# The last product of a decoder layer on one core: seven products of sums in place of direct rank-256 updates

## The chip, the cores and the metric

The kernel runs on one core of a Trainium2 chip. The metric is the device time of one execution in microseconds (us); of several runs the median counts. Data are 32-bit floats. TensorE works on pairs of a rounded high part and a low remainder ("hi" and "lo"): each product of two tiles is three matmuls, hi·hi, hi·lo and lo·hi.

## The reference, cut to what matters

One decoder layer over 1024 tokens of width 1024: two gated mixers (dilated attention and a spatial gating unit) with an output projection `w_out`, cross-attention into a memory, then a SwiGLU feed-forward layer and a final norm. The change concerns the feed-forward layer's second product, with D_FF = 2816:

```python
f = rmsnorm(h, g_ffn[l])
gt, up = jnp.split(f @ w_gate_up[l], 2, axis=-1)
h = h + (jax.nn.silu(gt) * up) @ w_down[l]
return rmsnorm(h, g_final)
```

## The kernel before

The 2816 hidden units are 22 blocks of 128 (`NJ`, index j). For every j the hidden tile `silu(gate)*up`, 128 units x 1024 tokens, is made and sent to DRAM (`hm_d`). Block 0 is made by plain products (`ff_plain`, L1309), the other 21 by `wino` (L416) with the class `Hidden` (L1328): seven products of sums of quarters (Strassen in Winograd's form), 12 matmuls of 512 columns each. The callbacks c11, c22, c12 and c21 turn the PSUM banks into the two halves of the tile `hmf` (tokens 0 to 511 and 512 to 1023); c12 (L1340) finishes the first half, c21 (L1350) the second, and then one DMA of SyncE's queue (SP) stores the tile (L1348).

`down` (L1357) then multiplies by `w_down`. It goes in nine groups of two hidden blocks and a last one of four (`FF_GROUPS`, L318). Of each block the hidden tile and 128 rows of the weight come through the staging pool `wst` (three buffers, L147), ScalarE (ACT) writes the hi part and VectorE (DVE) the lo part (`split`, L136 to L140). For each of 8 blocks of 128 tokens and each half of the 1024 columns, `mm3` (L166 to L171) accumulates a group in one PSUM bank, and a DVE addition adds it to the residual `h` (L1383). The last group adds the squares, the final norm and the stores (L1385 to L1402).

Tiles of 4 KB a partition come from `heap` (20 buffers), of 8 KB from `big` (8 buffers), split weights from `whl` (4 hi and 4 lo buffers). In the hidden stage `heap` holds 12 tiles of operand sums, three weight tiles for each of two blocks in work, and the `hmf` tiles.

The order of each engine's instructions is set by a scheduler ahead of time, which places what its model takes as ready. `keep_in_program_order` pins an instruction behind everything already traced on its engine. Each engine then works strictly in that order, and so do the DMA queues of SP, ACT and GpSimd (POOL): a DMA that waits holds up those behind it.

Two earlier places matter. `out_proj` (L1136) multiplies by `w_out`: its eight row blocks are loaded by SP through `wst` and split, and POOL loads eight tiles of `x` (L1143, pinned). After them POOL has nothing to do until the last group of `down` (L1362).

Of the kernel before, what the change touches and what calls it, by code (L numbers as in the profile page):

```python
# [85 lines left out]
def tile_hybrid_dilated_attn_sgu_gated_block(  # L86
# [169 lines left out]
    def plan_w(*items):  # L256
        plan.extend(items)
# [19 lines left out]
    def rows(w, k):  # L277
        return lambda: load_split([w[0, k * P:(k + 1) * P, :][:, None, :]], (1, 1024))
# [39 lines left out]
    FF_GROUPS = [(j, j + 1) for j in range(0, NJ - 4, 2)] + [tuple(range(NJ - 4, NJ))]  # L318
    hm_d = dram.tile([NJ, P, S], F32, name="hm_d")
    h_d = dram.tile([NT, P, D], F32, name="h_d")  # L320

    def ff_hidden(j):
        def go():
            t = BIG("hm", (P, 2, S))
            return load_split([hm_d[j][:, None, :]], (1, S), (t[:, 0], t[:, 1]))
        return go
# [3 lines left out]
    for js in FF_GROUPS:  # L330
        for jj in js:
            plan_w(ff_hidden(jj), rows(w_down, jj))

# [975 lines left out]
    def ff_plain(j):  # L1309
        wg, wu = next_w(0), next_w(0)  # L1310
        t = H("hmf")
        for half in range(2):
            order.join("f%d" % half)
            if half == 1:
                ready_w.append(next(start_w()))
                sums(lambda name, kk: raw_f[name][kk], "S1")
            hs = slice(half * HALF, (half + 1) * HALF)
            ps = []
            for w in (wg, wu):
                ps.append(PS("psg"))  # L1320
                yield from mm3(ps[-1], [(w[0][:, k], w[1][:, k], a_k(half, 0, k), a_k(half, 1, k))
                                        for k in range(NK)], T512)
                if w is wg:
                    nc.scalar.activation(t[:, hs], ps[0], AF.Silu)
            nc.vector.tensor_mul(t[:, hs], t[:, hs], ps[1])
        nc.sync.dma_start(hm_d[j], t)

    class Hidden:  # L1328
        def __init__(self, j):
            self.j = j  # L1330
            self.t = H("hmf")

        def c11(self, a):
            nc.scalar.activation(self.t[:, :HALF], a, AF.Silu)
# [5 lines left out]
        def c12(self, u, c):  # L1340
            nc.vector.tensor_add(u, u, c)
            nc.vector.tensor_mul(self.t[:, :HALF], self.t[:, :HALF], u)
            self.put()

        def put(self):
            self.n = getattr(self, "n", 0) + 1
            if self.n == 2:
                nc.sync.dma_start(hm_d[self.j], self.t)  # L1348

        def c21(self, p1, b):  # L1350
            t = self.t[:, HALF:]
            nc.vector.tensor_add(p1, p1, b)
            nc.scalar.activation(t, p1, AF.Silu)
            nc.vector.tensor_mul(t, t, self.up)
            self.put()

    def down(js, final=False):  # L1357
        if final:
            ng = H("ng")
            ap = bass.AP(tensor=g_final.tensor, offset=g_final.offset, ap=[[0, P], [1, D]])  # L1360
            tc.keep_in_program_order(nc.scalar.dma_start(ng, ap))
            nc.gpsimd.tensor_scalar(ng, ng, -1.0, None, op0=ALU.mult)  # L1362
        if js[0] == 0:
            for tb in range(NT):
                h[tb] = H("h")
                nc.sync.dma_start(h[tb], h_d[tb])
        wd = []
        for jj in js:
            hm[jj] = next_w(2)
            wd.append(next_w(2))  # L1370
        for tb in range(NT):
            ts = slice(tb * P, (tb + 1) * P)
            if final:
                y = H("y")
                ss = small.tile([P, 8], F32, name="ss", tag="ss")
            last = final and tb == NT - 1
            pieces = ((0, 512), (512, 256), (768, 256)) if last else ((0, 512), (512, 512))
            for i, (c0, n) in enumerate(pieces):
                ns = slice(c0, c0 + n)
                ps = PS("psd")[:, :n]  # L1380
                yield from mm3(ps, [(hm[j][0][:, 0, ts], hm[j][1][:, 0, ts], w[0][:, 0, ns], w[1][:, 0, ns])
                                    for j, w in zip(js, wd)], n / 512 * T512)
                nc.vector.tensor_add(h[tb][:, ns], h[tb][:, ns], ps)  # L1383
                if final:
                    nc.scalar.activation(y[:, ns], h[tb][:, ns], AF.Square, accum_out=ss[:, i:i + 1])  # L1385
            if not final:
                continue
            nc.vector.tensor_add(ss[:, 4:5], ss[:, 0:1], ss[:, 1:2])
            if last:
                nc.vector.tensor_add(ss[:, 4:5], ss[:, 4:5], ss[:, 2:3])  # L1390
            r = neg_rsqrt(ss[:, 4:5], 1)
            for n in range(2):
                ns = slice(n * 512, (n + 1) * 512)
                if last:
                    nc.vector.scalar_tensor_tensor(y[:, ns], h[tb][:, ns], r[:, 0:1], ng[:, ns],
                                                   op0=ALU.mult, op1=ALU.mult)
                    nc.sync.dma_start(out[0, tb * P:(tb + 1) * P, ns], y[:, ns])
                else:
                    nc.scalar.activation(y[:, ns], h[tb][:, ns], AF.Copy, scale=r[:, 0:1])
                    nc.gpsimd.tensor_mul(y[:, ns], y[:, ns], ng[:, ns])  # L1400
            if not last:
                nc.sync.dma_start(out[0, tb * P:(tb + 1) * P, :], y)  # L1402

    def main():
        yield from start()
        x_sums()
        yield from proj_v(2)
        yield from wino_rows(SV())
        for g, pr in QK_PAIRS:
            yield from wino(QK(g, pr))  # L1410
        for j in (0, 2):
            yield from wino(Act(AF.Gelu_apprx_tanh, (u_d[j], u_d[j + 1])))
        for j in range(GATES):
# [24 lines left out]
        order.join("combine")  # L1438
        yield from branch_attn()
        yield from out_proj()  # L1440
        yield from q_proj(0)
        spawn_cross(0)
        yield from q_proj(1)
        order.join("x0")
        spawn_cross(1)
        yield from cross_out(0)
        yield from cross_out(1)
        yield from ff_plain(0)
        for j in range(1, NJ):
            yield from wino(Hidden(j), plain_first=j == 1)  # L1450
        for js in FF_GROUPS:
            yield from down(js, final=js is FF_GROUPS[-1])

    order.run(main())

# [56 lines left out]
```

## Time and profile before

| | us |
|---|---|
| median of 3 runs | 1520.75 (1517.08 to 1521.48) |
| the profiled execution | 1518.75 |
| its span, first to last instruction | 1517.0 |
| PE busy | 1484.5 (98%) |
| DVE busy | 972.6 (64%) |
| ACT busy | 555.5 (37%) |
| POOL busy | 95.4 (6%) |

The mean granted clock of TensorE is 0.991 of full speed. The profiled execution is 1.75 us longer than its span and 2.0 us under the median. A busy share is an average over stages; which wait ends last has to be read stage by stage. "PE" are the matmuls, "PEld" the loads of the stationary operand beside them.

### The profile page before, as it was taken

The numbers are of one execution on the slowest core, as the hardware profiler recorded it, in microseconds if no ns is written. First come the engines' busy times: TensorE is split into PE (matmuls) and PEld (weight loads), VectorE is DVE, ScalarE is ACT, GpSimd is POOL, SyncE is SP. The second block draws the span as 40 slices with busy tenths as digits, with TensorE's granted clock in tenths as the row PEclk, the third lists the DMA queues.
The fourth block names the chain that finished last, engine by engine and source line by source line (L and its number), as shares of the span: only waits on it lengthen the run. The fifth ranks groups of instructions, "written<-read, shape, count | busy, mean of one in ns | idle before, by whom it ended". The sixth has DMA issues, their size and how long they took to land.

```text
span 1517.0 us, 19581 instructions
## 1 busy us (share of the span) xinstructions
PE 1484.5 (98%) x7567; PEld 1244.8 (82%) x7567; DVE 972.6 (64%) x1789; ACT 555.5 (37%) x1028; POOL 95.4 (6%) x107
## 2 busy tenths in 40 slices
PE   8999999999998999899999999999999999999997
PEld 8899888888886777788888888888888888888886
DVE  7786555555456848626677995555555546766666
ACT  4245233333346851215456732222222222211124
POOL 5300000000012203000000000000000000000014
PEclk9999999999999999999999999999999999999999
DMA  6223333333396429300111232222222226332312
GB/s 213 66 90 119 111 111 111 111 111 111 112 310 225 171 86 307 123 1 13 57 56 70 84 102 84 84 81 84 83 83 82 83 98 251 122 99 85 97 56 98
DMA packets 135634, 168.54 MB, mean 111 GB/s; under 512 B 7742, under 2 KB 108850, under 8 KB 135412
## 3 DMA queue, kind: packets, MB, share of 16 engines
q1 hardware_dynamic: 122304, 125.04, 25.7%
q0 software_dynamic: 8096, 29.13, 5.7%
q10 hardware_dynamic: 5140, 13.11, 2.5%
q8 instruction: 59, 0.97, 0.3%
q14 instruction: 35, 0.29, 0.1%
HBM read 125.17 MB, written 42.09 MB: 110 GB/s over the span
## 4 chain that ended last, share of the span: by engine, by line
PE 87%; DVE 5%; DMA 4%; ACT 2%; issue 1%; POOL 0%; SPq 0%; DVEq 0%; ACTq 0%; POOLq 0%
PE psb L412 20%; PE psc L412 13%; PE psg L412 13%; PE psd L171 5%; PE psd L169 5%; PE psd L170 5%; PE pso L171 3%; PE pso L169 3%; PE pso L170 3%; PE psv L170 1%; PE psv L169 1%; PE psv L171 1%; PE psb L491 1%; DMA wbc<-wt_d 1%; DMA wst<-in_w_in_dram 1%
## 5 line engine op out<-in xcount | busy, mean ns | idle before, releaser
L137 ACT ACTIVATE wh<-wst 128x1024 fp32r<-128x1024 f32 x134 | 140.3, 1056 | 411.4 <-PE psg L412 245.8
L140 DVE TENSOR_TENSOR wl<-wst,wh 128x1024 fp32r<-128x1024 f32 x130 | 160.8, 1240 | 80.3 <-ACT wh L137 80.0
L412 PE MATMUL psg<-A,wh 128*128 128x512 f32 x592 | 182.4, 389 | 0.0
L1383 DVE TENSOR_TENSOR h<-h,psd 128x512 f32<-128x512 f32 (+1 forms) x161 | 108.1, 681 | 60.0 <-PE psd L171 59.8
L171 PE MATMUL psd<-wh,hm 128*128 128x512 f32 (+1 forms) x356 | 137.6, 387 | 0.0
L170 PE MATMUL psd<-wl,hm 128*128 128x512 f32 (+1 forms) x356 | 137.6, 387 | 0.0
L169 PE MATMUL psd<-wh,hm 128*128 128x512 f32 (+1 forms) x356 | 137.5, 387 | 0.0
L412 PEld LDWEIGHTS psg<-A,wh 128*128 128x128 f32 x592 | 111.0, 188 | 23.0
L412 PE MATMUL psg<-A,wl 128*128 128x512 f32 x296 | 115.1, 389 | 0.0
L412 PE MATMUL psc<-S,t 128*128 128x512 f32 x444 | 106.6, 389 | 0.0
L412 PEld LDWEIGHTS psc<-S,t 128*128 128x128 f32 x444 | 83.3, 188 | 17.3
L412 PE MATMUL psc<-S,wh 128*128 128x512 f32 x296 | 91.4, 390 | 0.0
L412 PE MATMUL psb<-S,wh 128*128 128x512 f32 x296 | 91.2, 389 | 0.0
L412 PE MATMUL psb<-S,t2h 128*128 128x512 f32 x296 | 91.1, 389 | 0.0
L412 PE MATMUL psb<-A,t2h 128*128 128x512 f32 x288 | 88.7, 389 | 0.0
L433 DVE TENSOR_TENSOR u<-p,psb 128x512 f32<-128x512 f32 x37 | 25.4, 686 | 92.9 <-PE psb L412 92.9
L170 PEld LDWEIGHTS psd<-wl,hm 128*128 128x128 f32 x356 | 66.8, 188 | 14.1 <-DVE wl L140 0.3
L171 PEld LDWEIGHTS psd<-wh,hm 128*128 128x128 f32 x356 | 66.9, 188 | 13.6
L169 PEld LDWEIGHTS psd<-wh,hm 128*128 128x128 f32 x356 | 66.8, 188 | 13.5
L436 DVE TENSOR_TENSOR v<-p,psc 128x512 f32<-128x512 f32 x37 | 25.4, 686 | 64.1 <-PE psc L412 64.1
L137 ACT ACTIVATE t2h<-wst 128x1024 fp32r<-128x1024 f32 x37 | 39.3, 1061 | 72.1 <-DVE wst L398 53.7
L412 PEld LDWEIGHTS psg<-A,wl 128*128 128x128 f32 x296 | 55.6, 188 | 11.6
(344 smaller groups left out, 3270.9 us busy)
## 6 DMA issues: line engine op xcount, KB each, us to landing
wst<-in_w_gate_up_dram SPq DMA_DIRECT2D x44, 512.0 KB, 4.0
wst<-in_w_in_dram SPq DMA_DIRECT2D x42, 512.0 KB, 4.7
hm_d<-hmf SPq DMA_DIRECT2D x22, 512.0 KB, 4.4
wst<-hm_d SPq DMA_DIRECT2D x22, 512.0 KB, 3.4
wst<-in_w_down_dram SPq DMA_DIRECT2D x22, 512.0 KB, 3.7
sig_d<-act ACTq DMA_DIRECT2D x16, 512.0 KB, 3.4
xin<-in_x_dram SPq DMA_DIRECT2D x8, 512.0 KB, 8.6
wst<-in_w_kv_cross_dram SPq DMA_DIRECT2D x8, 512.0 KB, 5.0
```

The source lines that it names most:

```text
L137: i = nc.scalar.activation(hi, src, AF.Copy)
L140: (eng or nc.vector).tensor_sub(lo, src, hi.bitcast(F32))
L169: nc.tensor.matmul(ps, lhsT=lh, rhs=rh, start=(i == 0), stop=False)
L170: nc.tensor.matmul(ps, lhsT=lh, rhs=rl, start=False, stop=False)
L171: nc.tensor.matmul(ps, lhsT=ll, rhs=rh, start=False, stop=(i == n - 1))
L412: nc.tensor.matmul(ps, lhsT=l, rhs=r, start=first and k == 0 and i == 0, stop=k == 3 and i == 2, skip_group_check=not first)
L433: nc.vector.tensor_add(u, p1, b)
L436: nc.vector.tensor_add(v, p1, c)
L491: nc.tensor.matmul(p, lhsT=l, rhs=r, start=first and t % 2 == 0 and k == 0 and i == 0, stop=k == 3 and i == 2, skip_group_check=not first ...
L1383: nc.vector.tensor_add(h[tb][:, ns], h[tb][:, ns], ps)
```

## The change

The hidden matrix A (1024 tokens x 2816) and `w_down` (2816 x 1024) are cut into quarters. The contraction's halves are the even and the odd hidden blocks (11 each, `KP`), the others are the two halves of the tokens ("lo_", "hi_") and of the output columns. Seven products of sums replace the eight direct ones. Each product is one stage of 11 steps over its whole contraction, in four PSUM banks (one for each 128 tokens); a step has 4 x 3 matmuls of 512 columns.

- Sums of hidden quarters are made by DVE: one subtraction at each odd block of the hidden stage (`Hidden.put`), for which the even block's tile is kept in `heap` for one block longer; the others in `prep` of the stages 0, 2 and 3.
- Sums of weight quarters (T1 to T4) are made in DRAM by 32 DMAs of POOL's queue, pinned behind `out_proj`: 16 plain copies and 16 that add to what is there. A sum of 2.75 MiB goes in four pieces of three or two blocks.
- Hidden tiles and `h` are loaded by POOL's queue, straight to SBUF; SP loads two weight blocks at a time. `prep` splits the operands; up to four steps are kept ready (`whl` has four buffers).
- The banks are read by `into`, in part after later stages have begun (`todo`, two calls a step). Two stages go on accumulating in the banks of an earlier one.
- `hm_d` is stored in halves, four DMAs of 256 KB for each pair of blocks.

```diff
-        nc.sync.dma_start(hm_d[j], t)
+            if half == 0:
+                nc.sync.dma_start(hm_d[j][:, hs], t[:, hs])
+        hm[j] = t
...
+        def put(self, half):
+            hs = slice(half * HALF, (half + 1) * HALF)
+            j = self.j
+            if half == 0 or j % 2:
+                nc.sync.dma_start(hm_d[j][:, hs], self.t[:, hs])
+            if half == 1 and j % 2:
+                e = hm.pop(j - 1)
+                nc.vector.tensor_sub(e[:, hs], e[:, hs], self.t[:, hs])
+                nc.sync.dma_start(hm_d[j - 1][:, hs], e[:, hs])
...
+    def down_sums():
+        for dst, src in (("T3", "W22"), ("T1", "W11"), ("T3", "W12"), ("T1", "W12"), ("T2", "T3"), ("T2", "W11"),
+                         ("T4", "T2"), ("T4", "W21")):
+            for k0, k1 in ((0, 3), (3, 6), (6, 9), (9, KP)):
...
+                tc.keep_in_program_order(nc.gpsimd.dma_start(
+                    wsum_d[dst][k0:k1].rearrange("k p c -> p k c"), s_, **({} if first_ else {"accum_op": ALU.add})))
...
+        place(0, (0, 1, 2), False)
+        place(0, (3, 4, 5, 6), True)
+        place(0, (7, 8, 9, 10), False)
+        place(1, (0, 1, 2, 3), True)
+        for tb in range(NT):
+            h[tb] = H("h")
+            nc.gpsimd.dma_start(h[tb], h_d[tb])
+        place(1, (4, 5, 6, 7), True)
+        place(1, (8, 9, 10), False)
...
+        stages = ((even, lo_, "W11"), (odd, lo_, "W21"), (even, lo_, "T2"), (even, hi_, "T1"), (odd, lo_, "W22"),
+                  (even, lo_, "T3"), (odd, hi_, "T4"))
...
+            split(a, hi[:, :HALF], lo[:, :HALF])
+            split(w, hi[:, HALF:], lo[:, HALF:])
...
+            if s_ == 0:
+                nc.vector.tensor_sub(e[:, lo_], e[:, hi_], e[:, lo_])
+            elif s_ == 2:
+                nc.vector.tensor_add(o[:, lo_], o[:, lo_], e[:, lo_])
+            elif s_ == 3:
+                nc.vector.scalar_tensor_tensor(e[:, lo_], o[:, hi_], -1.0, e[:, lo_], op0=ALU.mult, op1=ALU.subtract)
...
+                while n_prep < min(n0 + 4, len(steps)):
+                    prep(n_prep)
+                    n_prep += 1
+                for _ in range(2):
+                    if todo:
+                        todo.pop(0)()
+                for t in range(4):
+                    ts = slice(t * P, (t + 1) * P)
+                    for k in block:
...
+                        for i, (l, r) in enumerate(((ah, wh), (ah, wl), (al, wh))):
+                            nc.tensor.matmul(bank[t], lhsT=l, rhs=r, start=fresh and i == 0,
+                                             stop=k == KP - 1 and i == 2, skip_group_check=s_ > 3)
...
         yield from out_proj()
+        down_sums()
```

## Rows read from the trace of the kernel before

**Rows 1.** The page's head: busy time of the engines.

```profile
span 1517.0 us, 19581 instructions
...
PE 1484.5 (98%) x7567; PEld 1244.8 (82%) x7567; DVE 972.6 (64%) x1789; ACT 555.5 (37%) x1028; POOL 95.4 (6%) x107
```

**Rows 2.** Stretches: length, each engine's busy time (instructions), granted clock, DMA share, GB/s.

```profile
640.00:680.00 40.00, 40.00 (x178) 33.11 (x177) 9.87 (x21) 5.09 (x14) 0.00 (x0) 1.00 0.01 1
...
1000.00:1100.00 100.00, 100.00 (x442) 82.78 (x442) 60.01 (x80) 27.73 (x37) 0.00 (x0) 1.00 0.27 86
...
1280.00:1400.00 120.00, 120.00 (x531) 99.38 (x530) 84.69 (x112) 24.36 (x24) 0.00 (x0) 1.00 0.32 101
```

**Rows 3.** Timeline at the first matmuls of `down`: start, duration, instruction.

```profile
1267.74 0.39 PE L169 MATMUL psd<-wh,hm 128*128 128x512 f32 x1
...
1267.97 0.39 PE L170 MATMUL psd<-wl,hm 128*128 128x512 f32 x1
...
1269.90 0.69 DVE L1354 TENSOR_TENSOR hmf<-hmf,v 128x512 f32<-128x512 f32 x1
```

**Rows 4.** Timeline at the end: the last matmul and the last DVE work.

```profile
1507.20 0.28 PE L170 MATMUL psd<-wl,hm 128*128 128x256 f32 x1
1507.32 0.28 PE L171 MATMUL psd<-wh,hm 128*128 128x256 f32 x1
...
1512.54 1.42 DVE L1395 SCALAR_TENSOR_TENSOR y<-h,ny,ng 128x512 f32<-128x512 f32 x2
```

**Rows 5.** Timeline of ACT and DVE in one block of the hidden stage.

```profile
1089.63 0.62 ACT L137 ACTIVATE t<-t1f 128x512 fp32r<-128x512 f32 x1
1090.43 0.68 DVE L140 TENSOR_TENSOR t<-t1f,t 128x512 fp32r<-128x512 f32 x1
1091.03 0.68 DVE L397 TENSOR_TENSOR wst<-wst,t1f 128x512 f32<-128x512 f32 x1
...
1096.35 1.22 DVE L140 TENSOR_TENSOR t2l<-wst,t2h 128x1024 fp32r<-128x1024 f32 x1
...
1099.59 0.34 SPq L1348 DMA_DIRECT2D hm_d<-hmf  x1
```

**Rows 6.** DMA issues of the whole run: count, KB each, median us to landing.

```profile
hm_d<-hmf SPq DMA_DIRECT2D x22, 512.0 KB, 4.4
...
sig<-sig_d POOLq DMA_DIRECT2D x8, 512.0 KB, 11.3
...
sv<-sv_d POOLq DMA_DIRECT2D x2, 1024.0 KB, 9.1
wst<-in_w_branch_sgu_dram SPq DMA_DIRECT2D x4, 512.0 KB, 11.0
```

**Rows 7.** POOL: its last load of `out_proj`, and its longest wait of the run.

```profile
611.49 0.53 POOL L1143 DMA_DIRECT2D h<-in_x_dram  x1 [1.92 <-DVE mg L1073]
...
POOL ng L1362 <- DMA ng<-in_g_final_dram: 833.0, 1, 833.0
```

**Rows 8.** Timeline of the start of `out_proj`.

```profile
618.39 3.79 SPq L147 DMA_DIRECT2D wst<-in_w_out_dram  x2
...
622.10 1.06 ACT L137 ACTIVATE wh<-wst 128x1024 fp32r<-128x1024 f32 x1 [12.35 <-DMA wst<-in_w_out_dram]
622.88 1.22 DVE L140 TENSOR_TENSOR wl<-wst,wh 128x1024 fp32r<-128x1024 f32 x1
...
624.02 1.42 DVE L140 TENSOR_TENSOR ml<-mg,mh 128x256 fp32r<-128x256 f32 x4
...
624.49 0.79 PE L171 MATMUL pso<-wo,ml 128*128 128x512 f32 x1 [4.73 <-DVE ml L140]
```

**Rows 9.** DMA issues of 576 to 577, 600 to 612 and 612 to 619 us: KB, us to landing.

```profile
wst<-in_w_out_dram SPq DMA_DIRECT2D x1, 512.0 KB, 8.9
...
wst<-in_w_out_dram SPq DMA_DIRECT2D x2, 512.0 KB, 6.8
...
wst<-in_w_out_dram SPq DMA_DIRECT2D x1, 512.0 KB, 3.6
```

More of the change, by code (lines that the diff above doesn't have):

```diff
@@ L317, in tile_hybrid_dilated_attn_sgu_gated_block @@
     plan_w(*[rows(w_o_cross, k) for k in range(MH)])
[L318 removed]
+    KP = NJ // 2
     hm_d = dram.tile([NJ, P, S], F32, name="hm_d")
     h_d = dram.tile([NT, P, D], F32, name="h_d")
[L322 to L326, printed above, removed]
+    wsum_d = {n: dram.tile([KP, P, HALF], F32, name=f"{n}_d") for n in ("T1", "T2", "T3", "T4")}
     plan_w(chunk(w_gate_up, 0), chunk(w_gate_up, FF))
     plan_wino(w_gate_up, *[(j * P, FF + j * P) for j in range(1, NJ)])
[L330 to L332 removed]
     QUARTERS = (("A11", "A12"), ("A21", "A22"))
@@ L1354, in c21 @@
             nc.vector.tensor_mul(t, t, self.up)
[L1355 to L1370, printed above, removed]
-        for tb in range(NT):
[L1372 to L1387, printed above, removed]
@@ new lines, in down, with hm_load, place, prep @@
+    def down():
+        even, odd = {}, {}
+        def hm_load(j, t):
+            (odd if j % 2 else even)[j // 2] = t
+            nc.gpsimd.dma_start(t, hm_d[j])
+        def place(which, ks, in_big):
+            for k in ks:
+                if not in_big:
+                    hm_load(2 * k + which, H("hm"))
+                elif k in (ks[0], ks[2]):
+                    two = big.tile([P, 2, S], F32, name="hm2", tag="b")
+                    hm_load(2 * k + which, two[:, 0])
+                    hm_load(2 * k + 2 + which, two[:, 1])
+        place(0, (0, 1, 2), False)
+        place(0, (3, 4, 5, 6), True)
+        place(0, (7, 8, 9, 10), False)
+        place(1, (0, 1, 2, 3), True)
+        for tb in range(NT):
+            h[tb] = H("h")
+            nc.gpsimd.dma_start(h[tb], h_d[tb])
+        place(1, (4, 5, 6, 7), True)
+        place(1, (8, 9, 10), False)
+        ng = H("ng")
+        ap = bass.AP(tensor=g_final.tensor, offset=g_final.offset, ap=[[0, P], [1, D]])
+        nc.gpsimd.dma_start(ng, ap)
+        nc.gpsimd.tensor_scalar(ng, ng, -1.0, None, op0=ALU.mult)
+        lo_, hi_ = slice(0, HALF), slice(HALF, S)
+        stages = ((even, lo_, "W11"), (odd, lo_, "W21"), (even, lo_, "T2"), (even, hi_, "T1"), (odd, lo_, "W22"),
+                  (even, lo_, "T3"), (odd, hi_, "T4"))
+        steps = [(s_, k) for s_ in range(7) for k in range(KP)]
+        wld, ready = {}, {}
+        def prep(n):
+            s_, k = steps[n]
+            tiles, part, wname = stages[s_]
+            if k % 2 == 0:
+                src = (WQ[wname] if wname in WQ else wsum_d[wname])[k:min(k + 2, KP)]
+                wld[s_] = load([src.rearrange("k p c -> p k c")])[0]
+            w = wld[s_][:, (k % 2) * HALF:(k % 2 + 1) * HALF]
+            a = tiles[k][:, part]
+            hi = whl.tile([P, 1024], F32R, name="wh", tag="hi")
+            lo = whl.tile([P, 1024], F32R, name="wl", tag="lo")
+            split(a, hi[:, :HALF], lo[:, :HALF])
+            split(w, hi[:, HALF:], lo[:, HALF:])
+            ready[n] = (hi, lo)
+            e, o = even[k], odd.get(k)
+            if s_ == 0:
[4 more added lines that the diff above has]
+                nc.vector.scalar_tensor_tensor(e[:, lo_], o[:, hi_], -1.0, e[:, lo_], op0=ALU.mult, op1=ALU.subtract)
+        def into(tb, c, op, ps):
+            cs = slice(c * HALF, (c + 1) * HALF)
+            op(h[tb][:, cs], h[tb][:, cs], ps)
+        add, sub = nc.vector.tensor_add, nc.vector.tensor_sub
+        todo = []
+        ys, ssq = {}, {}
+        def square(tb, c):
+            if c == 0 and tb % 2 == 0 and tb < 4 or c == 1 and tb % 2 == 0 and tb >= 4:
+                ys[tb // 2] = big.tile([P, 2, D], F32, name="y", tag="b")
+            if tb not in ssq:
+                ssq[tb] = small.tile([P, 8], F32, name="ss", tag="ssf", bufs=4)
+            y = ys[tb // 2][:, tb % 2]
+            cs = slice(c * HALF, (c + 1) * HALF)
+            nc.scalar.activation(y[:, cs], h[tb][:, cs], AF.Square, accum_out=ssq[tb][:, c:c + 1])
+        def finish(tb):
+            y = ys[tb // 2][:, tb % 2]
+            ss = ssq[tb]
@@ L1401, in down @@
-            if not last:
-                nc.sync.dma_start(out[0, tb * P:(tb + 1) * P, :], y)
+            for c in ((0, 1) if tb < 4 else (1, 0)):
+                cs = slice(c * HALF, (c + 1) * HALF)
+                if tb < 4:
+                    nc.scalar.activation(y[:, cs], h[tb][:, cs], AF.Copy, scale=r[:, 0:1])
+                    nc.gpsimd.tensor_mul(y[:, cs], y[:, cs], ng[:, cs])
+                elif c == 1:
+                    nc.scalar.activation(y[:, cs], y[:, cs], AF.Copy, scale=r[:, 0:1])
+                else:
+                    nc.vector.scalar_tensor_tensor(y[:, cs], h[tb][:, cs], r[:, 0:1], ng[:, cs],
+                                                   op0=ALU.mult, op1=ALU.mult)
+                if tb == NT - 1:
+                    (nc.sync if c == 0 else nc.scalar).dma_start(out[0, tb * P:(tb + 1) * P, cs], y[:, cs])
@@ new lines, in finish, with done, rest @@
+            if tb < NT - 1:
+                nc.sync.dma_start(out[0, tb * P:(tb + 1) * P, :], y)
+        def done(s_, t, ps):
+            u, l = t, 4 + t
+            if s_ == 0:
+                todo.extend((lambda: into(u, 0, add, ps), lambda: into(u, 1, sub, ps),
+                             lambda: into(l, 0, add, ps), lambda: into(l, 1, sub, ps)))
+            elif s_ == 1:
+                todo.append(lambda: into(u, 0, add, ps))
+            elif s_ == 2:
+                into(u, 1, sub, ps)
+            elif s_ == 3:
+                into(l, 1, add, ps)
+            elif s_ == 4:
+                into(u, 1, add, ps)
+                todo.extend((lambda: square(u, 0), lambda: square(u, 1), lambda: finish(u)))
+            elif s_ == 5:
+                into(l, 1, sub, ps)
+                def rest():
+                    square(l, 1)
+                    y = ys[l // 2][:, l % 2]
+                    nc.gpsimd.tensor_mul(y[:, HALF:], h[l][:, HALF:], ng[:, HALF:])
+                todo.append(rest)
+            else:
+                into(l, 0, add, ps)
+                square(l, 0)
+                finish(l)
@@ new lines, in down @@
+        banks = {}
+        n_prep = 0
+        for s_ in range(7):
+            name = "psx" if s_ in (0, 2, 5, 6) else "psy"
+            if s_ in (0, 1, 2, 3):
+                banks[name] = [PS(name) for _ in range(4)]
+            bank = banks[name]
+            tail = 4 if s_ == 6 else 2
+            blocks = [[k] for k in range(KP - tail)] + [list(range(KP - tail, KP))]
+            for block in blocks:
+                n0 = s_ * KP + block[0]
+                while n_prep < min(n0 + 4, len(steps)):
[7 more added lines that the diff above has]
+                    for k in block:
+                        hi, lo = ready[s_ * KP + k]
+                        ah, al, wh, wl = hi[:, ts], lo[:, ts], hi[:, HALF:], lo[:, HALF:]
+                        fresh = s_ in (0, 1, 2, 3) and k == 0
+                        for i, (l, r) in enumerate(((ah, wh), (ah, wl), (al, wh))):
+                            nc.tensor.matmul(bank[t], lhsT=l, rhs=r, start=fresh and i == 0,
+                                             stop=k == KP - 1 and i == 2, skip_group_check=s_ > 3)
+                        yield 3 * T512, 0.0
+                    if block[-1] == KP - 1:
+                        done(s_, t, bank[t])
@@ L1450, in main @@
             yield from wino(Hidden(j), plain_first=j == 1)
-        for js in FF_GROUPS:
-            yield from down(js, final=js is FF_GROUPS[-1])
+        yield from down()
     order.run(main())
```

24 lines of the change are left out of this document (9 added, 15 removed).

## The prediction

> **What bounds the kernel now.** I read the head of the page first: PE is busy for 98% of the span, DVE for 64%, ACT for 37%, POOL for 6% [rows 1]. That is a mean over many stages, so the table of stretches came next. In the hidden stage and in `down` PE is busy for the whole of each stretch at a granted clock of 1.00, while DVE has 40% and 29% free, ACT 72% and 80%, and POOL does nothing [rows 2]. So at the place of the change only a smaller number of matmuls can shorten the span, as long as what feeds them keeps up.
>
> The timeline gives the length of `down`. Its first matmul starts at 1267.74, with no gap behind the hidden stage, and its last starts at 1507.32 [rows 3, 4]. Of its 1068 matmuls 1044 have 512 columns and 24 have 256 (the last token block works in halves); the 24 start 0.12 us apart [rows 4], 2.9 us in all. 1507.44 - 1267.74 = 239.7; without 2.9 that is 236.8 for 1044, 0.2268 us each. Two neighbours start 0.23 apart [rows 3], and 100 us of the hidden stage hold 442, 0.2262 each [rows 2]. I use 0.2265. The product is dense: there is no idle time in it to win. Then follow 9.6 us of tail, 1507.4 to 1517.0: the last additions, the norm, and two outputs of DVE from 1512.54 on [rows 1, 4].
>
> **The change, part by part.**
>
> *Matmuls.* 7 stages x 11 steps x 12 = 924 of 512 columns. At 0.2265 us that is 209.3 us (the two readings of the pitch differ by 0.6 over it). Against 239.7: **-30.4 us**. The stationary and moving shapes stay, so the pitch should.
>
> *Splits and sums in the last stage.* For 512 columns DVE instructions last 0.68 us and start 0.60 us apart when they follow each other; an ACT split lasts 0.62 [rows 5]. A step of PE is 12 x 0.2265 = 2.72 us. ACT needs 1.24 of it. DVE needs two low parts, and in stages 0, 2 and 3 one sum: 1.80. Stage 1 is the worst, since 16 bank readings of stage 0 come two a step beside the two low parts: 4 x 0.60 = 2.40 by the starts, 2.72 by the durations. That is 88 to 100% of the step, for eight of 77 steps, with up to four steps prepared ahead. I cost DVE at nothing; the cover is the prepared steps, and at the upper end DVE is only level with PE. The bound is 0 to 5 us (0.6 us for each of the eight steps, if the four do not overlap at all and wait for each other). It is nearest to 0, since the starts at 0.60 are rows of just this kind of work.
>
> *Tail.* One 512-wide output of DVE goes to ACT (0.7 us less), but DVE has to finish four norms within the last block instead of one each 5.4 us. I take 9.6 us as before, between -1.5 and +2.
>
> *The hidden stage.* A subtraction for each pair of blocks adds 11 x 0.60 = 7 us of DVE where it is 40% free [rows 2]: nothing. Of each pair of blocks SP now stores four times 256 KB in place of twice 512, and a store that waits for DVE holds up the weight loads behind it; those are for the next block but one, so they have a block of cover (19 us): nothing. The even tile is kept for one block longer, and `heap` has just 20 places: 12 sums, 6 weight tiles, 2 hidden tiles. A third hidden tile, that of the next even block, finds room only when the two before are stored. The store leaves 3.1 us after the next block's start (1099.59 against 1096.5, nine blocks of 84 x 0.2265 = 19.03 us back from 1267.74) and takes 4.4 us [rows 3, 5, 6], so 1104.0; with a subtraction and a second store ahead, some 1106. The tile is first written when that block's four first products are done, 4 x 2.72 = 10.9 us after its start, 1107.4. Slack 1.4 us, and the weights behind are prepared a whole block ahead (its last low part at 1096.35 belongs to a block that starts at 1115.5 [rows 5]). I cost it at nothing, with a bound of 0 to 3 us for each of ten even blocks: a rival below.
>
> *The sums of weights.* POOL's queue issues its last load of `out_proj` at 611.49 and later stands idle for 833 us in one piece [rows 7]. The 32 DMAs are pinned right behind, and nothing holds back the first eight (the copies into T3 and T1). So they start at 612, when SP is fetching the last two blocks of `w_out`. The first of these is issued at 618.39 and is on the path: ACT waits 12.35 us for it, DVE's low part and then `ml` stand behind ACT, and PE has waited 4.73 us when it goes on at 624.49 [rows 8]. This load took 3.6 us on quiet DMA engines. Loads of the same tensor took 6.8 beside POOL's loads, 8.9 in a crowded moment, and those of `w_branch_sgu` 11.0 [rows 6, 9]. So the load becomes 0 to 7.4 us longer, and PE's wait with it. I take 6.8, since there too POOL's plain loads are the other traffic: **+3.2 us**. The block after it has 18 matmuls of cover. Further on, from 640 to 680, the DMA engines are at 1% [rows 2], and the sums run there alone.
>
> *When the sums are done.* No row shows an accumulating DMA, nor one from DRAM to DRAM. A DMA of the sums holds 704 KB on average (2.75 MiB in four). From the nearest rows: 1024 KB in 9.1 us gives 6.3 for it, and 512 KB in 11.3 gives 15.5 [rows 6]. A copy takes 6.3 to 15.5; an adding one has three streams in place of two, 9.5 to 23.3. Even strictly one after the other, 16 x 15.5 + 16 x 23.3 = 621 us at the upper end: 612 + 621 = 1233. The queue must be free for the first hidden tile by about 1258 (4 to 7 us to land [rows 9], 2.5 us to split, for 1267.7). Four pieces run side by side, so I expect it free long before: nothing.
>
> The Trainium skill, "DMA: Bandwidth & Descriptors", section "Anatomy of one DMA — SWDGE (gpsimd) path", fits a GpSimd-issued DMA by 2.0 us plus its bytes at 436 GB/s, 3.2 us for 512 KB. The row above disagrees, with 11.3 us; by the page's estimate all 32 would take 117 us one after the other, and the rival of a late queue would have no place at all.
>
> *The start of the stage.* 22 hidden tiles and eight of `h`, 512 KB each, come through POOL's queue while the hidden stage runs out. The last even tile needs block 21's second half, which DVE finishes at 1270.6 [rows 3]; with the subtraction, a store of 4.4 and a load of 6.8 us [rows 6, 9], about 1283. It is split for step 10, three steps ahead of 1294.9, around 1287. The cover is 4 us; without it step 10 waits. Behind that load POOL's queue has the odd tiles and `h`; stage 1 needs them from 1297 on. Taken with the last block of stage 6, which needs four prepared steps at once: **+1.0 us**, between 0 and 6.
>
> *Sum.* -30.4 + 3.2 + 1.0 = -26.2 on the profiled execution's 1518.75: 1492.5. The median of the runs is 2.0 above that execution, within the spread of 4.4 us of the three. I forecast 1493.
>
> **The rivals.**
>
> *Slower: a late queue.* If a DMA that adds is much dearer than three streams, POOL is still waiting for sums when the hidden tiles are due. It decides from a mean spacing of (1258 - 612)/32 = 20.2 us a DMA, and each further microsecond costs 32; from 21.1 on the kernel is slower than before. With copies at 15.5 and additions at twice that, 16 x 15.5 + 16 x 31 = 744 us, free at 1356, 98 late: 1591. For it: no row has the price. Against: it takes each worst end, and no overlap. **0.12.**
>
> *The hidden stage pays for the kept tile.* Ten even blocks at up to 3 us: up to 1493 + 30 = 1523, 1508 at half that. For: 20 places for 21 tiles, and a store queue that is blocked by loads. Against: PE would feel it only after ACT and the banks fall behind. **0.10.**
>
> *The last stage is fed too slowly.* All bounds of its DVE, start and tail terms at once, 5 + 5 + 2, with the `w_out` load at its upper 7.4: 1493 + 16 = 1509. For: DVE without room in stage 1, 15 MB through one queue in some 40 us. **0.17.**
>
> *The change doesn't do what it says.* PE might keep as many matmuls by another count, or run them at a longer pitch since the bank changes every three. A pitch of 0.2585 us would give 238.9 us and no change, 1519 to 1524. Nothing in the rows speaks for it. **0.03.**
>
> **How the numbers follow.** The forecast case has 0.58, from 1487 (no contention, shorter tail) to 1500. To leave out no more than 2 in 10, the range takes in the slow feeding and half of the kept tile's case: 1486 to 1511. Of a measurement of this kernel about 0.3% (4.6 us) can be told from no change, so faster means under 1516. Faster: 0.58 + 0.17 and 0.06 of the kept tile, 0.81. Within: 0.03 and 0.02 of the kept tile, 0.05. Slower: the late queue and the last 0.02 of the kept tile, 0.14.
>
> **What would show it.** Right: 924 matmuls in seven stages of 29.9 us with PE busy throughout; the stretch of 616 to 628 with a longer wait for the `w_out` load; POOL's additions all landed before 1250; a hidden stage still at 19.0 us a block. Wrong: PE idle on `hm` or T2 with POOL's queue full; ACT waiting for a `hmf` buffer at even blocks, 38 us apart; DVE at 100% in stage 1 and PE waiting for low parts; matmuls further apart than 0.2265 us.

## The result, and the profile after

The changed kernel takes 1493.9 us (median of 4 runs, 1492.1 to 1499.3), the kernel before, run beside it, 1519.7: a ratio of 0.984, 95% interval 0.981 to 0.987. The forecast was 1493.0 in a range of 1486 to 1511. The profiled execution took 1492.1 us, with a span of 1490.4.

The head of the page and the table of stretches of the changed kernel (the columns are those of [rows 1] and [rows 2]; under the three stretches read before stand three of the last stage):

```profile
span 1490.4 us, 19516 instructions
...
PE 1458.7 (98%) x7423; PEld 1220.2 (82%) x7423; DVE 970.8 (65%) x1823; ACT 596.9 (40%) x1134; POOL 142.4 (10%) x168
```

```profile
640.00:680.00 40.00, 40.00 (x179) 33.10 (x178) 9.85 (x22) 4.41 (x13) 5.94 (x7) 1.00 1.09 236
1000.00:1100.00 100.00, 100.00 (x443) 82.81 (x442) 62.42 (x84) 28.52 (x37) 0.00 (x0) 1.00 0.27 85
1280.00:1400.00 120.00, 120.00 (x531) 99.36 (x530) 91.23 (x147) 53.01 (x96) 11.20 (x17) 1.00 0.49 171
...
1270.00:1300.00 30.00, 30.00 (x134) 24.82 (x134) 26.68 (x44) 12.67 (x22) 8.40 (x16) 1.00 0.99 379
1300.00:1330.00 30.00, 30.00 (x134) 24.85 (x133) 28.87 (x48) 13.95 (x27) 2.80 (x1) 1.00 0.61 222
...
1420.00:1451.00 31.00, 30.40 (x134) 24.51 (x133) 27.94 (x59) 19.98 (x39) 13.98 (x10) 1.00 0.47 161
```

PE is as full as before, with 144 matmuls fewer. In the last product its pitch is the old one (531 matmuls in 120 us, as in [rows 2]), and the hidden stage has its 100 us full again. The sums show in the first line: the DMA engines, idle there before, are full at 236 GB/s. DVE is at 96% in stage 1 and PE does not wait for it; the one stretch of the product with idle PE is that of stage 5, 30.40 of 31.

The timeline of the changed kernel at the first matmuls of the product and at the last one (rows 3 and 4 of before):

```profile
1270.05 0.39 PE L1526 MATMUL psx<-wh 128*128 128x512 f32 x1
...
1270.27 0.39 PE L1526 MATMUL psx<-wl,wh 128*128 128x512 f32 x1
...
1480.56 0.39 PE L1526 MATMUL psx<-wh,wl 128*128 128x512 f32 x1
```

From first to last start of a matmul that is 210.51 us against 239.58 [rows 3, 4]: -29.07. The product starts 2.31 us later than before: `out_proj` began 0.72 later (ahead of any edit), took 1.05 longer (its first matmul to the first of `q_proj`: 99.46 in place of 98.41), and another 0.54 came up to the last stage. The tail from the last matmul's start is 9.86 in place of 9.69. Together -26.6, the difference of the spans, 1517.0 and 1490.4.

DMA issues of the changed kernel (columns as in [rows 6]; first those of 612 to 760 us, then of the whole run):

```profile
T_d<-in_w_down_dram POOLq DMA_DIRECT2D x18, 768.0 KB, 15.0
T_d<-T_d POOLq DMA_DIRECT2D x6, 768.0 KB, 19.5
...
wst<-in_w_q_cross_dram SPq DMA_DIRECT2D x4, 512.0 KB, 26.6
...
wst<-in_w_out_dram SPq DMA_DIRECT2D x2, 512.0 KB, 8.8
...
hm_d<-hmf SPq DMA_DIRECT2D x44, 256.0 KB, 3.8
hm<-hm_d POOLq DMA_DIRECT2D x22, 512.0 KB, 8.8
```

POOL's timeline (the bracket is its idle time before, and what ended it): the first and last of the sums, the first hidden tiles, and the load of the last even tile:

```profile
612.73 5.88 POOL L1375 DMA_DIRECT2D T_d<-in_w_down_dram  x8
...
703.55 1.13 POOL L1375 DMA_DIRECT2D T_d<-in_w_down_dram  x1 [0.36 <-issue]
...
1253.96 2.20 POOL L1383 DMA_DIRECT2D hm<-hm_d  x4 [549.28 <-PE psg L404]
...
1280.79 0.53 POOL L1383 DMA_DIRECT2D hm<-hm_d  x1 [12.97 <-DMA hm_d<-hmf]
```

The queue issues 32 sums in 91 us, 2.9 us apart; the forecast set 20.2 us as the spacing from which it would be late. It is free 549 us before the first hidden tiles leave. A single sum took 15.0 to 19.5 us to land, with several under way at once. (The Trainium skill, "DMA: Bandwidth & Descriptors", section "Anatomy of one DMA — SWDGE (gpsimd) path", makes 3.8 us of 768 KB, an estimate; measured is 15.0. Its estimate for all 32, 117 us, is near: the DMA engines are quiet again at 716, 103 us after the first issue.)

The timeline of the start of `out_proj` in the changed kernel, against [rows 8]:

```profile
619.12 3.79 SPq L147 DMA_DIRECT2D wst<-in_w_out_dram  x2
...
622.47 1.22 DVE L1065 TENSOR_TENSOR mg<-mg,sig 128x1024 f32<-128x1024 f32 x1
...
623.61 1.22 DVE L140 TENSOR_TENSOR wl<-wst,wh 128x1024 fp32r<-128x1024 f32 x1
...
624.74 0.75 DVE L140 TENSOR_TENSOR ml<-mg,mh 128x256 fp32r<-128x256 f32 x2
...
625.22 0.70 PE L171 MATMUL pso<-wo,ml 128*128 128x512 f32 x1 [4.73 <-DVE ml L140]
...
628.26 1.06 ACT L137 ACTIVATE wh<-wst 128x1024 fp32r<-128x1024 f32 x1 [18.07 <-DMA wst<-in_w_out_dram]
...
629.23 0.71 ACT L137 ACTIVATE mh<-mg 128x256 fp32r<-128x256 f32 x2
...
629.68 0.50 PE L169 MATMUL pso<-wh,mh 128*128 128x512 f32 x1 [0.32 <-ACT mh L137]
...
630.34 1.22 DVE L140 TENSOR_TENSOR wl<-wst,wh 128x1024 fp32r<-128x1024 f32 x1
...
633.61 0.50 PE L170 MATMUL pso<-wl,mh 128*128 128x512 f32 x1 [0.76 <-DVE wl L140]
```

In the kernel before, the low part of this load's block is the first of these two, behind `ml`:

```profile
625.36 2.40 DVE L140 TENSOR_TENSOR wl<-wst,wh 128x1024 fp32r<-128x1024 f32 x2
```

The load that was issued at 619.12 is there at 628.26, 9.1 us later, where it had taken 3.7 (618.39 to 622.10). Yet PE's wait is 4.73 as before, because it never hung on this load. The low part ahead of `ml` (623.61 here, 622.88 in [rows 8]) is that of an earlier block: here it starts 4.65 us before the load is there, and before the change it starts 0.28 us before ACT is done with the high part of the load. From 617 us on DVE works without a gap up to `ml` in both kernels, so the wait is the length of DVE's own queue.

The late load is paid a little later. The high parts `mh` of the token block's second half stand behind it on ACT (629.23; 623.06 before), its low part comes at 630.34, and the next block's load is late too. PE waits for these operands four times between 628.97 and 633.61; from 628.97 to 634.41 its matmuls take 2.3 us more than the pitch.

Against the kernel before, part of this is hidden by TensorE's clock. The stretches of 624 to 628 and 628 to 632 us, first of the kernel before, then of the changed one (columns as in [rows 2]):

```profile
624.00:628.00 4.00, 3.51 (x8) 2.81 (x9) 4.00 (x8) 2.28 (x5) 0.00 (x0) 0.50 0.65 209
628.00:632.00 4.00, 4.00 (x14) 3.15 (x13) 1.10 (x4) 0.00 (x0) 0.00 (x0) 0.69 0.85 246
```

```profile
624.00:628.00 4.00, 2.78 (x7) 2.21 (x8) 1.50 (x3) 0.00 (x0) 2.22 (x3) 0.67 0.95 340
628.00:632.00 4.00, 3.65 (x14) 2.20 (x12) 1.90 (x3) 2.43 (x4) 1.45 (x2) 0.91 1.04 412
```

Around the end of PE's wait of 4.73 us the granted clock falls to half (1.2 GHz), and the matmuls start 0.43 us apart in place of 0.23. It stays there for 6.8 us in the kernel before (to 630.46) and for 3.4 in the profiled execution of the changed one (to 628.75). So the 1.05 us of `out_proj` are the price of the late loads less what the shorter slow stretch gives back; the profiles of the experiments separate the two (e2).

### The profile page after: what moved, and what is told of

Read it like the earlier page. It is cut to its first block, busy times and chain, and to the rows that moved or that the text cites. A ratio compares the mean times of both kernels' runs of the same rounds, so it can differ in the third digit from the quotient of the medians.

```text
span 1490.4 us, 19516 instructions
## 1 busy us (share of the span) xinstructions
PE 1458.7 (98%) x7423; PEld 1220.2 (82%) x7423; DVE 970.8 (65%) x1823; ACT 596.9 (40%) x1134; POOL 142.4 (10%) x168
## 4 chain that ended last, share of the span: by engine, by line
PE 85%; DVE 6%; DMA 4%; ACT 2%; issue 1%; SPq 1%; POOL 0%; ACTq 0%; DVEq 0%; POOLq 0%
PE psb L404 20%; PE psc L404 14%; PE psg L404 13%; PE psx L1526 6%; PE psy L1526 6%; PE pso L170 3%; PE pso L171 3%; PE pso L169 3%; PE psv L169 1%; PE psv L170 1%; DVE wl L140 1%; PE psv L171 1%; PE psb L483 1%; DMA wbc<-wt_d 1%; DMA wst<-in_w_in_dram 1%
## 5 line engine op out<-in xcount | busy, mean ns | idle before, releaser
L137 ACT ACTIVATE wh<-wst 128x1024 fp32r<-128x1024 f32 (+1 forms) x189 | 165.7, 878 | 363.1 <-PE psg L404 244.6
L140 DVE TENSOR_TENSOR wl<-wst,wh 128x1024 fp32r<-128x1024 f32 (+1 forms) x185 | 190.6, 1032 | 82.3 <-ACT wh L137 82.2
L137 ACT ACTIVATE wh<-hm 128x512 fp32r<-128x512 f32 x77 | 48.4, 630 | 97.0 <-PE psy L1526 46.0
L140 DVE TENSOR_TENSOR wl<-hm,wh 128x512 fp32r<-128x512 f32 x77 | 55.6, 722 | 45.0 <-ACT wh L137 44.8
L1526 PE MATMUL psx<-wl,wh 128*128 128x512 f32 x176 | 68.8, 391 | 0.6 <-DVE wl L140 0.6
L1526 PE MATMUL psx<-wh 128*128 128x512 f32 x176 | 68.5, 389 | 0.0
L1526 PE MATMUL psx<-wh,wl 128*128 128x512 f32 x176 | 68.5, 389 | 0.0
L1383 POOL DMA_DIRECT2D hm<-hm_d x22 | 11.7, 534 | 575.7 <-PE psg L404 549.3
L404 PEld LDWEIGHTS psb<-S,t2h 128*128 128x128 f32 x296 | 55.6, 188 | 11.6
L404 PEld LDWEIGHTS psb<-S,wh 128*128 128x128 f32 x296 | 55.5, 188 | 11.5
```

The source lines that it names most:

```text
L137: i = nc.scalar.activation(hi, src, AF.Copy)
L140: (eng or nc.vector).tensor_sub(lo, src, hi.bitcast(F32))
L404: nc.tensor.matmul(ps, lhsT=l, rhs=r, start=first and k == 0 and i == 0, stop=k == 3 and i == 2, skip_group_check=not first)
L1383: nc.gpsimd.dma_start(t, hm_d[j])
L1526: nc.tensor.matmul(bank[t], lhsT=l, rhs=r, start=fresh and i == 0, stop=k == KP - 1 and i == 2, skip_group_check=s_ > 3)
```

## The experiments

Account A is the sum of the prediction: what the change brings is fewer matmuls at an unchanged pitch, and what it costs is paid where its transfers meet other loads. The rivals are those that each expectation names. e1 to e4, e5 to e8, and e9 and e10 were each run beside the kernel before, whose medians were 1520.9, 1520.0 and 1520.1 us.

**e1, as changed.** No edit, the reference for e2 to e4.

> The changed kernel once more, as the measure for the next three. Account A (132 matmuls less are the gain; the sums cost 1 to 2 us around out_proj; GpSimd's products stall stage 5 by about 1.2 us) and its rivals alike: 1492 to 1499 us, stages 0 to 4 of the last product at 29.9 us each.

1492.4 us (1491.1 to 1496.0), ratio 0.983 [0.980, 0.985]. All stages are as in the first profile: five of 29.92, then 31.11 and 30.03 us.

**e2, no sums of weights.** The stages read plain quarters in place of T1 to T4.

```diff
-        down_sums()
...
-                src = (WQ[wname] if wname in WQ else wsum_d[wname])[k:min(k + 2, KP)]
+                src = WQ[{"T1": "W12", "T2": "W11", "T3": "W22", "T4": "W21"}.get(wname, wname)][k:min(k + 2, KP)]
```

> Leaves out the 32 DMAs that make the sums; the stages read plain quarters of w_down in their place, so only the values of the product change, not its matmuls. Account A: the w_out load lands after some 3.6 us, out_proj's first block is 1 to 2 us shorter, all else as it was: 1 to 2 us less than the changed kernel. Rival B (the sums' traffic also slows the loads of later stages and is paid in many small pieces): 4 us less or more.

1490.4 us (1489.6 to 1491.9), ratio 0.981 [0.979, 0.983]: 2.0 us less than e1, as account A has it; rival B falls. `out_proj` takes 97.22 us, against 99.46 in the first profile of the changed kernel and 99.71 in e1: its two loads land in 3.4 us (8.8 in the changed kernel). The product is as in e1, stage 5 included. PE's wait for `ml` is 4.73 us here too.

How much of this is the sums depends on the slow stretch of the clock. Without sums at this place `out_proj` took 96.93 to 97.22 us where the stretch at 1.2 GHz lasted 3.4 us (e2, e5, e8, e10) and 98.18 to 98.51 where it lasted 6.8 (the kernel before, e3, e6, e9). With them it took 99.45 to 99.53 (3.4 us, three profiles) and 99.71 (6.8 us, e1): there PE waits for the late blocks anyway. So the 22 MiB of sums cost 2.2 to 2.6 us beside a short slow stretch and 1.2 to 1.5 beside a long one, all of it in `out_proj`. What decides between the two lengths stays open.

**e3, the sums a little later**, where the DMA engines looked idle: POOL first reads one column that `out_proj` ends with.

```diff
+        gate = small.tile([P, 8], F32, name="gate", tag="gate", bufs=1)
+        tc.keep_in_program_order(nc.gpsimd.tensor_scalar(gate[:, 0:1], h[0][:, D - 1:D], 1.0, None, op0=ALU.mult))
         down_sums()
```

> The sums wait for the end of out_proj's first token block (a one-column GpSimd instruction reads it), when all of w_out is loaded. Account A: they start near 635 us in place of 613, out_proj gets back its 1 us, and nothing else changes: 0.5 to 2 us less than the changed kernel. Rival B: the traffic meets the loads of cross-attention instead, and the time is the same or longer.

1505.5 us (1503.3 to 1508.4), ratio 0.991 [0.988, 0.993]: 13 us slower than e1. Account A falls; rival B, the meeting with the loads of cross-attention, is what happened, though it named no price. In the profiled execution, the slowest of the four, the hidden stage begins at 861.82 in place of 845.52. The timelines of SP and ACT show the cause; first e1, then e3, where the sums start at 640 and the last leave at 722.81:

```profile
719.49 0.37 SPq L147 DMA_DIRECT2D wst<-in_w_q_cross_dram  x1
...
723.38 1.06 ACT L137 ACTIVATE wh<-wst 128x1024 fp32r<-128x1024 f32 x1 [1.36 <-DMA wst<-in_w_q_cross_dram]
```

```profile
718.96 0.37 SPq L147 DMA_DIRECT2D wst<-in_w_q_cross_dram  x1
...
722.81 1.14 POOL L1375 DMA_DIRECT2D T_d<-in_w_down_dram  x1 [0.42 <-issue]
...
737.14 1.06 ACT L137 ACTIVATE wh<-wst 128x1024 fp32r<-128x1024 f32 x1 [15.65 <-DMA wst<-in_w_q_cross_dram]
```

The fourth load of `w_q` can only leave when its buffer comes free, at 719, and ACT needs it almost at once. On quiet engines it takes 4 us, behind the last sums 18; PE then stands 14.6 us, and the granted clock is 0.50 from 730.49 to 747.56, partly behind the wait. In the changed kernel the sums are down at 716: it missed this by some 3 us.

**e4, no products of GpSimd in the norm** of the first four token blocks.

```diff
-                    nc.scalar.activation(y[:, cs], h[tb][:, cs], AF.Copy, scale=r[:, 0:1])
-                    nc.gpsimd.tensor_mul(y[:, cs], y[:, cs], ng[:, cs])
+                    nc.vector.scalar_tensor_tensor(y[:, cs], h[tb][:, cs], r[:, 0:1], ng[:, cs],
+                                                   op0=ALU.mult, op1=ALU.mult)
```

> The final scaling of the first four token blocks goes from ScalarE and GpSimd to VectorE, one instruction in place of two. Account A (a GpSimd product of two SBUF operands holds VectorE up for about 1.1 us): VectorE's low parts in stage 5 stay at 0.69 us in place of up to 1.78, stage 5 is 29.9 to 30.3 us in place of 31.1, the time 0.8 to 1.2 us less. Rival C (VectorE has simply too much work in stage 5): with 6 us more on it the stage becomes longer, 31.5 us or more.

1490.5 us (1489.5 to 1491.5), ratio 0.981 [0.979, 0.983], 1.9 under e1. Stage 5 takes 29.92 us, 1.2 less, and the span is 1.1 us shorter; the rest of the 1.9 is not in stage 5. Rival C falls: DVE has more to do here, and the stage is shorter. What was there without the edit, in the changed kernel's timeline:

```profile
1434.36 5.00 POOL L1462 TENSOR_TENSOR y<-y,ng 128x512 f32<-128x512 f32 x3 [0.36 <-ACT y L1461]
...
1434.72 1.78 DVE L140 TENSOR_TENSOR wl<-wst,wh 128x512 fp32r<-128x512 f32 x1
...
1436.43 1.78 DVE L140 TENSOR_TENSOR wl<-hm,wh 128x512 fp32r<-128x512 f32 x1
...
1436.56 0.50 PE L1526 MATMUL psx<-wl,wh 128*128 128x512 f32 x1 [0.21 <-DVE wl L140]
...
1439.97 0.50 PE L1526 MATMUL psx<-wl,wh 128*128 128x512 f32 x1 [0.39 <-DVE wl L140]
```

While POOL multiplies, a low part of DVE lasts 1.78 us in place of 0.68, and POOL's three products 1.67 each, where two in a row took 2.54 before the change. Four such low parts (the first at 1428.72), and four one-column instructions of the norm that take 1.15 to 1.34 us in place of 0.2, use up the steps prepared ahead. (The Trainium skill, "SBUF — State Buffer", section "Who interferes with whom": a DVE instruction with two SBUF inputs and a GpSimd instruction that reads SBUF hold each other up. The trace agrees; a low part and a product are such a pair.)

**e5 and e6, the sums in the hidden stage**, behind block 13 or 17: these price the forecast's rivals of the kept tile and the late queue.

```diff
         del hm[j]
+                if j == 13:   # e6: 17
+                    gate = small.tile([P, 8], F32, name="gate", tag="gate", bufs=1)
+                    tc.keep_in_program_order(nc.gpsimd.tensor_scalar(gate[:, 0:1], self.t[:, S - 1:S], 1.0, None,
+                                                                     op0=ALU.mult))
+                    down_sums()
...
-        down_sums()
```

> All 32 sum DMAs wait for hidden block 13, done near 1118 us, so that they run beside the weight loads of the hidden stage. They took 105 us behind out_proj. Account A (they only have to be issued before about 1258, and the hidden stage has a block of slack in its weights): last landing by 1245, no wait of PE in the hidden stage, out_proj as without sums, 1489 to 1492 us. Rival B (a plain load beside adding DMAs takes 18 us and more, as one did at the end of the last run, and a hidden block feels it): PE waits in the hidden stage, 1495 us or more.

> The same, behind hidden block 17, near 1194 us: with 105 to 130 us the queue is free at 1300 to 1325, 42 to 67 us after the hidden tiles are wanted. The rival of the prediction (a late queue) priced in the open: PE idle at the start of the last product for 40 to 75 us, 1530 to 1567 us. Against it: should the queue let the first tiles through earlier, under 1510.

e5: 1528.4 us (one run), and the hidden stage 34.5 us longer (458.98, in e1 424.43). Its waits from 1115 to 1310 us (total, times, longest):

```profile
PE psb L404 <- DVE v L1350: 27.5, 3, 17.0
DVE t1f L387 <- DMA wst<-in_w_gate_up_dram: 23.8, 3, 11.2
...
ACT hmf L1346 <- DMA hm_d<-hmf: 16.8, 1, 16.8
```

The last line is the kept tile: ACT has no buffer for a new even tile until the stores are out, and these stand behind weight loads that now take 10.2 us (4.2 over the whole run of the changed kernel). ACT's wait ends at 1197.21, and PE's longest, 17.0 us, at 1201.95. PE is idle for 27.6 us of the hidden stage in all, and the granted clock of the stage is 0.967, where it was 1.00 in e1. Account A, that the sums are hidden anywhere, fell; rival B's account of the loads held.

e6: 1531.0 us (one run), at the lower edge of what was expected. Here the last sum leaves at 1290.68, and its timeline shows the hidden tiles right behind; then its waits:

```profile
1290.68 1.14 POOL L1380 DMA_DIRECT2D T_d<-in_w_down_dram  x1 [0.44 <-issue]
1291.42 2.58 POOL L1388 DMA_DIRECT2D hm<-hm_d  x4
```

```profile
ACT wh L137 <- DMA hm<-hm_d: 32.7, 1, 32.7
...
PE psx L1531 <- ACT wh L137: 25.9, 1, 25.9
```

The first tiles left at 1253.96 in the changed kernel and leave 37.5 us later here; the product starts at 1306.73, 36.7 later. So the late queue works as the rival said, at about one us a us; 25.9 us of it are PE's wait for the tile, and 8.5 are a wait that came before, in the hidden stage. In the changed kernel the sums are 549 us away from it.

**e7, two of the three matmuls a tile**, to find DVE's limit. The product with the low part of the stationary operand is left out.

```diff
-                        for i, (l, r) in enumerate(((ah, wh), (ah, wl), (al, wh))):
+                        for i, (l, r) in enumerate(((ah, wh), (ah, wl))):
...
```

> Leaves out the product of the low part of the hidden tile with the high part of the weight: 616 matmuls in the last product in place of 924; all splits, sums and DMAs stay. A step of PE is 1.81 us. Account A (only the matmuls bound the stages; VectorE has room): stages of 20 us, but stage 1 bound by VectorE at 2.40 us a step, about 24; 145 to 155 us in all for 210.7, 1427 to 1440 us. Rival C (the feeding is nearly the bound already): stages of 25 us and more, over 1460 us.

1448.6 us (one run); the product takes 166.6, between the two bands. PE alone would need 19.9 us a stage; the stages took 24.3, 23.9, 23.0, 24.8, 20.1, 28.5 and 22.1. The stretches of e7, stages 2, 3 and 4:

```profile
1318.00:1341.00 23.00, 21.01 (x90) 16.14 (x89) 23.00 (x39) 15.66 (x31) 0.00 (x0) 1.00 0.43 124
1341.00:1366.00 25.00, 22.20 (x91) 17.56 (x90) 25.00 (x43) 13.68 (x24) 0.00 (x0) 0.93 0.46 139
1366.00:1386.00 20.00, 20.00 (x89) 16.52 (x90) 16.88 (x28) 12.02 (x23) 0.00 (x0) 1.00 0.50 147
```

In stages 2 and 3 DVE is busy without a gap and sets the time: its own limit is 23 to 25 us a stage. With twelve matmuls a step (29.9 us) that leaves 5 to 7 us of room in each; stage 4, with no sum to make, is at PE's limit again. Stage 1, the forecast's worst, took 23.9 with DVE busy for 93% of it, but PE's longest wait there, 3.2 us, was ended by ACT, so it is not shown to be DVE's. Account A missed its band by stages that it held to be PE's: over its 20 us a stage, 3.0 and 4.8 us are stages 2 and 3, 8.5 are stage 5 with the norm in it (e4), and 4.3 stage 0, which was not followed. Rival C's band, above 1460, held too little room for DVE.

**e8, the sums paced**, two behind each hidden tile of blocks 1 to 16, with e4's edit: in `put`, after the store,

```diff
+            if half == 1 and sums_left:
+                gate = small.tile([P, 8], F32, name="gate", tag="gate", bufs=1)
+                tc.keep_in_program_order(nc.gpsimd.tensor_scalar(gate[:, 0:1], self.t[:, S - 1:S], 1.0, None,
+                                                                 op0=ALU.mult))
+                for _ in range(2):
+                    sums_left.pop(0)()
...
```

> Two sum DMAs at the end of each of the hidden blocks 1 to 16, in place of 32 in a row behind out_proj, and the four first token blocks scaled by VectorE alone. Account A: out_proj as without sums (2.5 us less than the changed kernel), stage 5 at 29.9 us (1.2 less), no wait in the hidden stage: 1488 to 1490 us, 3 to 4 us under the changed kernel. Rival B: two adding DMAs at a time delay a block's weight loads by more than their slack, 1493 us or more.

1491.5 us (1490.9 to 1495.3), ratio 0.981 [0.980, 0.983], just above the expected band. `out_proj` took 96.93 us and stage 5 29.92, both as expected; one wait of PE in the hidden stage, ended by DVE, cost 1.1, and in the profiled run `out_proj` began 2.4 us later than in e1, ahead of every edit.

**e9, 24 sums later and eight paced.** If the fourth `w_q` load is what e3 paid for, e3 without its last eight sums pays nothing. So e3's gate, then 24 sums; the last eight go one a block with e8's lines, behind blocks 1 to 8 (block 0 has no `put`).

> As in the third run the sums wait for out_proj's accumulator read, but only the first 24 of them are issued there; the last eight (T4's copy and its addition) go one at a time behind the hidden tiles of blocks 0 to 7. Account A (the 13 us lost in the third run were the fourth w_q load, issued at 719 into the last eight sums): the first 24 are issued from 640 to about 700 and have landed before 719, ACT's wait for that load is back at 1 to 3 us, out_proj takes 97 us as without the sums, and the median is 1489 to 1492. Rival D (the third run lost its time to the later start as such, whichever transfers are still under way): ACT still waits over 10 us for w_q and the median stays above 1500.

1491.7 us (1490.1 to 1494.0), ratio 0.981 [0.979, 0.982]: 14 us under e3. ACT's timeline at the load, behind the last of the 24:

```profile
704.34 1.37 POOL L1384 DMA_DIRECT2D T_d<-in_w_down_dram  x1 [0.93 <-DMA T_d<-T_d]
...
725.40 1.06 ACT L137 ACTIVATE wh<-wst 128x1024 fp32r<-128x1024 f32 x1 [1.32 <-DMA wst<-in_w_q_cross_dram]
```

The wait of 15.65 is 1.32 again. Rival D, the later start as such, falls. `out_proj` took 98.36 where 97 was expected. The difference goes with the clock: it is granted at 0.50 from 627.46 to 634.29, 6.8 us, where in e10, with the same sums, it is so for 3.4 and `out_proj` takes 96.96.

**e10, e9 with e4's edit.**

> The run before it, with the two-input products of GpSimd in stages 5 and 6 done by DVE as in the fourth run. Account A: stage 5 takes 29.9 us in place of 31.1, and the median is 1488 to 1491, 1 to 2 us under the run before it. If GpSimd's products were not what delays stage 5, both medians agree within 0.5 us.

1489.2 us (1487.0 to 1489.4), ratio 0.979 [0.977, 0.981], 2.5 under e9. `out_proj` 96.96, stage 5 29.92, span 1487.2. The two profiled executions differ by 4.9 us of span: `out_proj` begins 2.5 us earlier than in e9 and is 1.4 shorter, with its shorter slow stretch, both ahead of the edit, and stage 5 is 1.2 shorter. So the edit's own share is 1.2, as expected, and not the whole 2.5. It is the fastest version that computes the whole product; against the first profile of the changed kernel it saves 2.5 us in `out_proj` and 1.2 in stage 5.

## Why the prediction was right

The main term and its mechanism were right. That 1493.0 came within 1 us of 1493.9 is luck as well: against the terms of the sum, the product gained 1.3 us less, `out_proj` cost 2.15 less and the start 1.0 less, and a loss of 1.4 lies in no term or in the tail.

**Matmuls: right.** 924 of 512 columns, as said, in 210.7 us of stages where 209.3 were forecast; five stages are 29.92, the forecast pitch. The surplus is stage 5's 1.2.

**Splits and sums: right at nothing in stages 0 to 3, with a reason that e7 confirms.** DVE alone needs at most some 25 us of a stage's 29.9, so the bound of 0 to 5 us was too wary. But the 1.80 us a step of stages 2 and 3 (19.8 a stage) were too few: e7's rows hold 39 and 43 DVE instructions, where the step counts 33, since bank readings fall there too. What the step left out is that the norm of four token blocks now lies inside stage 5, POOL's products with it: +1.2 us, shown by e4 and again by e10.

**`out_proj`: that the load meets the sums was right, the wait was wrong, and the size came out small by luck.** The step read the wait of 4.73 us as one for the load of 618.39, since a low part and `ml` follow ACT's row at 622.10 [rows 8]. That low part is an earlier block's, and the wait is DVE's queue: it stayed at 4.73 with the load at 9.1 us (above the forecast's 6.8, within its bound) and in e2 with the load on quiet engines. The price came from the operands behind the load, and the cover of 18 matmuls did not hold for the next block, whose low part PE waited for at 633.61. Measured where +3.2 was taken: +1.05 against before, with the clock's shorter slow stretch in it; at slow stretches of equal length 2.2 to 2.6 (short) or 1.2 to 1.5 (long).

**"The sums run there alone": wrong, and nearly dear.** The step looked at the DMA share of 640 to 680 [rows 2], and not at which load would come next. One on the path leaves at 719, and the sums end at 716. e3 prices the miss at 13 us, which would have given 1507; e9 shows that the load is the cause. No rival of the prediction held this; rival B of e3's expectation did.

**When the sums are done: right, far from its bound.** 2.9 us apart in place of at most 19.4. The late queue's price of about one us a us is what e6 shows.

**The kept tile: 0 us, as costed**, with PE full from 1000 to 1100. That the mechanism exists is shown by e5: ACT waits 16.8 us for one tile as soon as the store queue is crowded. It was right to hold it as a rival.

**Start of the stage: nothing where +1.0 was taken.** The load of the last even tile left at 1280.79, behind 13 us of waiting for its store; ACT split the tile at 1289.29 (forecast: around 1287), and what ended its wait there was PE, not the load. The cover of three steps held.

**Tail: 9.9 us, as said.** The 0.72 us ahead of `out_proj` and the 0.54 up to the last stage are in no term. The first is of the size by which executions differ: with nothing edited ahead of it, the first matmul of `out_proj` came between 619.3 and 623.7 over the experiments. Of the second 0.1 to 0.5 stands in the profiles of e1, e2, e4 and e7 as well, where nothing of that stretch is edited; its cause was not followed.

## What to carry to other kernels

A large transfer put beside other work has a price that depends on which load of the path it meets: list the loads that leave within its whole duration, by the time when their buffers come free, and not the mean DMA share of the stretch. Where it meets one, move only the part that does: in e9 eight of 32 made the difference of 14 us. Before a wait is put down to a late load, find in the rows which block each split belongs to; and compare two runs of a stage only where TensorE's clock was low for equally long. Where work comes into the shadow of an engine with little room, look also at what its neighbour does with the same memory: two-input instructions of DVE and GpSimd each became longer.

## What the runs showed of the hardware

- DMAs from DRAM to DRAM, plain and adding, run side by side: 16 of each kind, 512 or 768 KB, in 103 us. That is 22 MiB at some 220 GB/s, with all DMA engines busy. One of them lands in 15 to 20 us in that crowd.
- A plain 512 KB load issued into that backlog waits for much of it: 8.8 us (`w_out`), 18 (`w_q` in e3), 26.6 (median of `w_q`), against 3.4 (`w_out`) and 4.3 (`w_q`) in e2.
- A low part of DVE beside a product of GpSimd: 1.78 us in place of 0.68. One-column instructions of DVE with two inputs: 1.15 to 1.34 in place of 0.2.
- Behind a wait of PE of 4.7 us in `out_proj` the granted clock was 0.50 (1.2 GHz) for 3.4 us in seven profiles and for 6.8 in five (the kernel before, e1, e3, e6, e9). Matmuls of 512 columns start 0.427 us apart there and 0.227 at 2.4 GHz; without sums beside it `out_proj` is 1.0 to 1.6 us longer with the longer stretch.
